# A two-layer hybrid decoder step: cache copies behind the weights of the last layer's feed-forward, the decoded tokens' old conv columns packed into rows before their store

## The chip, the core and the metric

The kernel runs on one core of a Trainium2 chip. The metric is the device time of one execution in microseconds (us). A core has a matrix engine (TensorE, PE in the profile; its weight loads are listed apart as PEld), a vector engine (VectorE, DVE), a scalar engine (ScalarE, ACT), a general engine (GpSimd, POOL) and a sync engine (SyncE, SP), which issues this kernel's transfers to 16 DMA engines. Each engine works through its own list of instructions in order; what it issues to a queue is served beside it. Operands lie in the on-chip SBUF (128 partitions), products are summed up in PSUM, inputs and outputs lie in DRAM.

## The reference, cut to what matters

Two layers work on 1048 tokens: 16 meta tokens and a prompt of 1024, and eight sequences that decode one token each. The numbers are float32.

```python
def decoder_layer(x, lp, st, prompt):
    hn = rmsnorm(x, lp['ln1'])
    q, k, v, u, z, xbc, dtr = split(hn @ lp['w_in'])   # dtr: four columns
    o_att, nk, nv = ...            # window attention over 128 keys; a decoded token's come from the caches
    y5, s5r, s5i = s5_scan(u, ...)                     # S5 state space
    xbc, nconv = causal_conv(xbc, conv0, w, bias)      # four taps; the state is the last three columns
    yc, hssd = ssd_scan(xs, softplus(dtr + bias), ...) # Mamba-2 SSD
    x = x + concat(norm(o_att), norm(y5), norm(yc)) @ lp['w_out']
    return x + (silu(h2 @ wg) * (h2 @ wu)) @ wd        # h2 = rmsnorm(x, lp['ln2'])
# outputs of a decoded token, per layer:
#   k_s, v_s: the cache without its oldest key and value, and the new one
#   conv_s:   the two newer of the three old conv columns, and the new one
```

The older part of k_s and v_s (`o_ko`, `o_vo`: 127 of 128 rows of 128 numbers, for eight sequences and two layers) and of conv_s (`o_convo`: two columns of 512 features for eight sequences, per layer) is only copied from inputs.

## The kernel before, in words

Features lie on partitions, tokens on columns. The tokens are cut into two halves of 528 and 520 columns (`TH`), each half into chunks of 264 and 264 or 256 (`CH`). The program calls the two halves' phases of each layer in an interleaved order: projections and feed-forward (`in_proj`, `out_proj`, `ffn`), which keep PE full, beside the mixers (`attn`, `s5`, `ssd`).

A matrix of weights comes as tiles of 128 x 1024 numbers, 0.52 MB. `weights` loads one into `wr` (two buffers); ACT casts it to `wh` and DVE subtracts to get the rest, `wl` (lines 181 and 183; three buffers each). `mm3` (lines 203 to 210) makes each product in three passes: high part by high part, by low part, and low part by high part, so 24 matmuls a chunk in a projection. For the four columns of dt both parts of the weights share one pass (`weights_dt`), 16 matmuls a chunk.

`load` (line 118) issues every transfer, in or out, on SP, so all stand in one queue. The code's order isn't the order on the engines: a scheduler places each instruction by its dependencies and priority, the weight loads with a priority that lets them go ahead.

At the start the eight tiles of the residual `x` are loaded in chunks (`load_x`); ACT squares them (line 222, `add_square`), the squares are summed, and for the norm factor ACT copies a PSUM row out (line 230, `rstd_sum`). Each product of the first projection is multiplied by this factor on DVE (line 344 in `in_proj`, 348 for other tiles), which frees its PSUM buffer for PE.

The decoded tokens' conv state of a layer is loaded as `cst8` (line 835), 128 partitions of 4 tiles x 8 sequences x 3 columns, in the half that holds the decoded tokens; `ssd` uses it and line 864 stores its newer two columns as they lie there: 4 x 8 x 128 = 4096 runs of two numbers. `ssds` (line 913) is a small tile of `ssd`, copied by DVE before a product with it.

The cache copies (four `load` calls near the program's end, just ahead of the last two `ffn` calls) go from DRAM to DRAM, four in all, each eight rows of 127 x 128 numbers, 65 KB a row. They depend on nothing, and the scheduler places them at the start, ahead of the loads of x.

`ffn(1, 0, na, between)` is the feed-forward of layer 1, first half: for three groups of hidden tiles (8, 8 and 6), `ffn_up` and then `ffn_down`, which takes eight weight tiles `m` and adds their products to x. The S5 products of layer 1, second half (lines 742 to 757), run beside it; they load matrices from DRAM (`ds5d`).

Of the kernel before, what the change touches and what calls it, by code (L numbers as in the profile page):

```python
# [21 lines left out]
DEPTH = 2  # L22
FH = 2816
NHID = FH // 128
TH = (528, 520)            # columns of the two token halves
T0 = (0, 528)
NPR = (528, 512)           # prompt columns of each half
CH = (((0, 264), (264, 528)), ((0, 264), (264, 520)))
CHN = (((16, 272), (272, 528)), CH[1])      # without the meta tokens
NK8 = (66, 64)             # chunks of eight tokens in each half  # L30
# [5 lines left out]
def build(ctx, tc, A):  # L36
# [25 lines left out]
    def slot():  # L62
        # scratch [128, 528]; while the dense phases leave their tiles free these stand in
        if lend["from"] != "s":
            t = lend["half"]
            if t is not None:
                lend["half"] = None
                return t
            t = lent("hs")
            lend["half"] = t[:, 1].bitcast(F32)  # L70
            return t[:, 0].bitcast(F32)
        return slp.tile([128, 528], F32, tag="s", name=nm("s"))
# [4 lines left out]
    def rounded2():  # L77
        # two of them for operands of one-pass products
        if lend["from"] != "s":
            t = lent("hr")  # L80
            return t[:, 0], t[:, 1]
        return [slp.tile([128, 528], F32R, tag="s", name=nm("r")) for _ in range(2)]

    def together(*jobs):
        # steps of the jobs in turn: (generator, where its scratch comes from, its banks)
        alive = list(jobs)
        while alive:
            for job in list(alive):
                g, lend["from"], lend["psum"] = job
                if next(g, job) is job:  # L90
                    alive.remove(job)
        lend.update({"from": "s", "half": None, "psum": "o"})
# [24 lines left out]

    def load(out, in_):
        nc.sync.dma_start(out=out, in_=in_)  # L119
# [20 lines left out]
    # keys: part of the partitions' half, group, other part  # L140
    kp2 = const([128, 2, 2, 640], "kp2", F32R)
    # states of S5 with their real parts above the imaginary ones
    hz = const([128, 4, 2, 67], "hz")
    sz = const([128, 8, 2, 8], "sz")
    # running sums of SSD: rows of three bfloat16 parts, and what picks one of the rows
# [40 lines left out]
    def weights_dt(l, mi):  # L186
        # only four columns: their second parts stand beside the first ones and share a pass
        raw = wp.tile([128, 8, 128], F32, tag="wr", name=nm("wr"), bufs=2)
        with tc.high_priority(offset=3000):
            load(raw, A["w_in"][l, mi])  # L190
        wh = wp.tile([128, 8, 128], F32R, tag="wh", name=nm("wh"))
        S.copy(wh, raw)
        wl = wp.tile([128, 8, 128], F32R, tag="wl", name=nm("wl"))
        S.copy(wl, raw)
        V.tensor_sub(wl[:, :, 32:36], raw[:, :, 0:4], wh[:, :, 0:4].bitcast(F32))
        return wh, wl
# [36 lines left out]
    def rstd_diag(acc, n, scale):  # L233
        # 1 / sqrt(scale * column sums + eps), tokens on partitions, on the diagonals of squares
# [13 lines left out]
    def rstd_rows(acc, n, scale):  # L248
        # the same on all partitions
        w, dg = rstd_diag(acc, n, scale)  # L250
        ps = pmx()
        PE.matmul(ps[:, :n], ones[0:w, :], dg[0:w, :n], start=True, stop=True)  # L252
        return ps[:, :n]
# [46 lines left out]
    def in_norm(l, hf, new):  # L300
        # the gains go on here, the tokens' factors on the products
# [13 lines left out]
    def in_proj(l, hf, xr, early=0):  # L315
        # early: for so many tiles the banks that attention does not use yet serve too
# [4 lines left out]
        for mi, name in enumerate(MT):  # L321
            w = weights(A["w_in"][l, mi], 8) if name != "dt" else weights_dt(l, mi)
            st = stp.tile([128, 528], F32, tag="st", name=nm("st"))
            for c0, c1 in CH[hf]:
# [38 lines left out]
    S5 = {}  # L363

    def s5_prep(l):
# [69 lines left out]
        # abar and its powers 0..8  # L435
# [28 lines left out]
        # zero-order hold  # L464
# [33 lines left out]
        # unit rotations e^{i 8 phi (k+1)} and the decay of a chunk  # L498
# [42 lines left out]
        # chunk matrices  # L541
# [7 lines left out]
        # rows (group, channel) that meet their own channel, for the direct path  # L549
# [3 lines left out]
        # powers in falling order for the chunk's own states  # L553
# [3 lines left out]
        # the inputs' matrices of a pair of groups, apart  # L557
# [7 lines left out]
        for p in range(0, 8, 2):  # L565
# [46 lines left out]
            # convolution kernel inside a chunk: (distance, channel out) by (group, channel in) ...  # L612
# [7 lines left out]
            if p % 4 == 2:  # L620
                # ... turned, with the direct path, and written once for every step
# [11 lines left out]
        # each row moved on by its own step: from a row to the next the reading starts 16 earlier  # L633
# [7 lines left out]
    def s5(l, hf):  # L641
# [6 lines left out]
        nu = nk + 16 if dec else nk     # columns of a group: chunks, and the decoded tokens in first and in last place  # L648
# [11 lines left out]
        for r in range(2):  # L660
# [43 lines left out]
            if dec:  # L704
                # state of the decoded token
# [74 lines left out]
        # gelu, gate, norm; the columns stay in chunk order until the last step  # L780
# [45 lines left out]
    def ssd(l, hf):  # L826
# [10 lines left out]
        for i, name in enumerate(("xs0", "xs1", "B", "C")):  # L837
# [8 lines left out]
            for j in range(3):  # L846
                a = 0 if hist else 3 - j        # the first columns of a prompt have less history
                V.scalar_tensor_tensor(ac[:, a:NP], xi[:, a + hist - 3 + j:NP + hist - 3 + j],
                                       cw[:, 4 * i + j:4 * i + j + 1], ac[:, a:NP], ALU.mult, ALU.add)
# [13 lines left out]
        if dec:  # L863
            load(A["o_convo"][l], cst8[:, :, :, 1:3])
# [9 lines left out]
        # step sizes, tokens on partitions  # L874
# [39 lines left out]
        # the same as rows, in three parts without a rest  # L914
# [20 lines left out]
        # decay of a whole chunk on the partitions of its group  # L935
# [8 lines left out]
        for c0, nq, bi in blocks:  # L944
# [20 lines left out]
            # decay between tokens of the chunk  # L965
# [50 lines left out]
        # gate and norm  # L1016
# [11 lines left out]
    def ssd_dec(l, X, Bt, Ct, dt, dA, yt):  # L1028
# [8 lines left out]
        # step and decay of each head on its partitions  # L1037
# [42 lines left out]
    def attn(l, hf):  # L1080
# [6 lines left out]
        # keys, rotated; the block before the half stands in front  # L1087
# [10 lines left out]
        # both parts of the keys of a group, each on both halves of the partitions  # L1098
# [51 lines left out]
        def rope(c0, nq):  # L1150
# [11 lines left out]
            # the parts of a group's queries, one above the other  # L1162
# [7 lines left out]
        def geometry(c0, nq, bi):  # L1170
            # key columns [before | own]: number before, first column, number, first mask column
# [8 lines left out]
        def scores(blk, qav, jp):  # L1180
            # heads 4 v + j for two j: one bank for both j of a v
# [33 lines left out]
        def values(blk, ps_, jp, po_):  # L1215
            c0, nq, bi = blk
            nb, k0, nkk, m0 = geometry(*blk)
            # a group's two heads: over the keys before and over the own ones
# [130 lines left out]
    def out_proj(l, hf, seq=range(8), banks=None):  # L1349
        # seq: the parts in the order in which they come; banks: of the mixers, when these have come to their end  # L1350
# [3 lines left out]
        for i in seq:  # L1354
# [4 lines left out]
            if j < 4:  # L1359
                # the gains of attention's norm go on here  # L1360
# [6 lines left out]
        # the first columns of the last features come earlier, for the norm that follows  # L1367
# [38 lines left out]
    def ffn_down(l, hf, hs, grp, ms=range(8)):  # L1406
        g0, g1 = grp
        for m in ms:
            w = weights(A["w_down"][l, m, :, g0:g1, :], g1 - g0)
            for c0, c1 in chunks_of(l, hf):  # L1410
# [5 lines left out]
    def ffn(l, hf, xn, between=None):  # L1416
        for grp in HGROUPS:
# [5 lines left out]
            elif (l, hf) == (DEPTH - 1, 1) and grp is HGROUPS[-1]:  # L1423
                ffn_end(hs, grp)
            else:
                ffn_down(l, hf, hs, grp)

    def ffn_end(hs, grp):
        # the last products, and the final norm chunk after chunk
# [69 lines left out]
    for l in range(DEPTH):  # L1499
        load(A["o_ko"][l], A["ck"][l, :, 1:128, :])  # L1500
        load(A["o_vo"][l], A["cv"][l, :, 1:128, :])
    late = []

# [4 lines left out]
    ffn(1, 0, na, between)  # L1508
# [25 lines left out]
def _host(i):  # L1534
# [16 lines left out]
    # four columns only, the rest of their tile is empty  # L1551
    wcols["dt"] = np.concatenate([wcols["dt"], np.zeros((2, 1024, 124), f)], axis=2)

    def tiles(w, nm_):
        # (L, K, M) -> (L, m tile, k within, k tile, m within)
# [13 lines left out]
    def feat(a, n):  # L1569
        # (L, n*128) -> (128, L, n)  # L1570
# [10 lines left out]
    P["cw"] = i["ssd_conv_w"].reshape(2, 4, 4, 128).transpose(3, 0, 2, 1)   # l j tile p -> p l tile j  # L1581
# [6 lines left out]
    sd = np.tile(i["attn_sinks"], (1, 16)).T               # 128 rows of (b kv r)  # L1588
    P["sinkd"] = sd

    def gn(a):
        # (L, 16 g, 64 n, ...) -> (128 = (g%2, n), L, 8 pairs, ...)
# [8 lines left out]
                          i["s5_c_im"].transpose(0, 1, 3, 2))]     # each 128 L pair c  # L1601
# [3 lines left out]
    # states  # L1605
    st = np.stack([i["state_s5_re"], i["state_s5_im"]], axis=1)     # l e b g n
    st = st.reshape(2, 2, 8, 8, 2, 64).transpose(0, 4, 5, 1, 3, 2)  # l h n e pair b
    r["s5st"] = c(st.reshape(2, 128, 2, 8, 8))
    r["cstate"] = c(i["state_ssd_conv"].reshape(2, 8, 3, 4, 128).transpose(0, 4, 3, 1, 2))
    ss = i["state_ssd"].reshape(2, 8, 2, 2, 64, 64).transpose(0, 2, 3, 4, 1, 5)  # l t h p b n  # L1610
# [6 lines left out]
    # constants of the shapes  # L1617
# [64 lines left out]
```

## Time and profile before

| what | us |
|---|---|
| median of three timed runs | 2535.39 |
| lowest and highest | 2534.82, 2536.57 |
| span of the profiled execution | 2540.2 |
| PE idle in it | 112 |

The profile is of one execution; its own time is the span. A busy matmul is one that the record shows between start and end; the matmuls overlap, so their mean duration is longer than the distance between two. In a timeline, a number in brackets is how long the engine had stood idle before the instruction and what ended that. In windows, each engine has its busy us and its instructions, then the clock granted to PE (1.00 is 2.4 GHz, 0.50 is 1.2 GHz), the busy share of the DMA engines and what they moved; in a short window the DMA share can come out above 1.

In forty equal slices of the span, PE is busy in tenths, and the clock granted to it:

```profile
PE   4899887999999999999999999999999999999998
PEclk7999898999999999999999999999999999999999
```

### The profile page before, as it was taken

What the parts mean: (1) busy time and instruction counts of PE and PEld (TensorE: products, weight loads), DVE (VectorE), ACT (ScalarE), POOL (GpSimd) and SP (SyncE); (2) the same over time, 40 slices, a digit from 0 to 9 for tenths busy, and PEclk for the clock granted to TensorE, in tenths of its full rate; (3) what the DMA queues carried; (4) which work ended last, traced back from release to release, by engine and by line L of the source; (5) the groups of instructions that cost most, each with busy time, mean ns of one, the idle gap of its engine ahead of it and who ended that gap; (6) DMA issues with size and microseconds to landing.
All of it is one profiled execution on the core that took longest, in us unless ns stands there. A gap on an engine that the chain in (4) does not pass through costs nothing.

```text
span 2540.2 us, 49614 instructions
## 1 busy us (share of the span) xinstructions
PE 2428.5 (96%) x19878; PEld 2339.0 (92%) x19878; DVE 1460.9 (58%) x3502; ACT 1052.3 (41%) x2177; POOL 350.8 (14%) x476
## 2 busy tenths in 40 slices
PE   4899887999999999999999999999999999999998
PEld 4898787899999999999999999999999998999997
DVE  4886646665557645665654455666565446434435
ACT  4364633334444443443553343333455335323224
POOL 3521112011111231001200022001110004000000
PEclk7999898999999999999999999999999999999999
DMA  8655345354323624344422233435433232332322
GB/s 175 214 189 153 94 136 70 94 166 139 105 85 111 195 93 144 105 133 119 130 84 92 88 116 117 140 109 158 149 96 92 84 121 91 110 92 92 93 89 78
DMA packets 210645, 301.06 MB, mean 119 GB/s; under 512 B 63840, under 2 KB 140464, under 8 KB 210384
## 3 DMA queue, kind: packets, MB, share of 16 engines
q1 hardware_dynamic: 210416, 297.91, 39.2%
q8 instruction: 156, 2.56, 0.4%
q14 instruction: 73, 0.60, 0.1%
HBM read 255.86 MB, written 46.17 MB: 119 GB/s over the span
## 4 chain that ended last, share of the span: by engine, by line
PE 77%; DVE 9%; issue 5%; DMA 4%; SPq 2%; ACT 2%; POOL 1%; DVEq 0%; POOLq 0%; ACTq 0%
PE pb L208 22%; PE pb L209 22%; PE pb L210 22%; SPq L119 2%; DVE wl L183 2%; PE px L1241 1%; PE px L1196 1%; DVE xn L262 1%; PE px L754 1%; DMA s<-dq 1%; PE px L757 1%; DMA x<-xt 1%; DVE hh L201 1%; PE px L1244 1%; PE px L252 1%
## 5 line engine op out<-in xcount | busy, mean ns | idle before, releaser
L208 PE MATMUL pb<-hh,wh 128*128 128x264 f32 (+1 forms) x3200 | 919.3, 287 | 18.6 <-DVE th L1400 16.1
L209 PE MATMUL pb<-hh,wh 128*128 128x264 f32 (+1 forms) x3200 | 913.3, 285 | 0.8 <-DVE hh L201 0.8
L210 PE MATMUL pb<-hh,wl 128*128 128x264 f32 (+1 forms) x3200 | 911.7, 285 | 0.0
L208 PE MATMUL pb<-hl,wh 128*128 128x264 f32 (+1 forms) x2304 | 666.0, 289 | 43.2 <-DVE st L344 26.1
L209 PE MATMUL pb<-hl,wh 128*128 128x264 f32 (+1 forms) x2304 | 663.2, 288 | 0.6 <-DVE hl L1363 0.4
L210 PE MATMUL pb<-hl,wl 128*128 128x264 f32 (+1 forms) x2304 | 661.0, 287 | 0.0
L208 PEld LDWEIGHTS pb<-hh,wh 128*128 128x128 f32 x3200 | 607.7, 190 | 29.3 <-DVE th L1400 20.2
L181 ACT CAST wh<-wr 128x512 fp32r<-128x512 f32 (+2 forms) x536 | 387.1, 753 | 555.1 <-PE pb L209 512.4
L210 PEld LDWEIGHTS pb<-hh,wl 128*128 128x128 f32 x3200 | 607.3, 190 | 3.5 <-issue 2.7
L209 PEld LDWEIGHTS pb<-hh,wh 128*128 128x128 f32 x3200 | 606.3, 189 | 3.0 <-DVE hh L201 1.1
L183 DVE TENSOR_TENSOR wl<-wr,wh 128x512 fp32r<-128x512 f32 (+2 forms) x536 | 461.1, 882 | 179.0 <-ACT wh L181 172.9
L208 PEld LDWEIGHTS pb<-hl,wh 128*128 128x128 f32 x2304 | 441.1, 192 | 53.2 <-issue 33.0
L209 PEld LDWEIGHTS pb<-hl,wh 128*128 128x128 f32 x2304 | 440.5, 191 | 4.5 <-issue 2.3
L210 PEld LDWEIGHTS pb<-hl,wl 128*128 128x128 f32 x2304 | 440.6, 191 | 1.1 <-issue 0.6
L225 POOL TENSOR_TENSOR sq<-sq,sq 128x264 f32<-128x264 f32 (+1 forms) x142 | 117.4, 832 | 760.1 <-ACT sq L222 661.9
L1414 DVE TENSOR_TENSOR x<-x,pb 128x264 f32<-128x264 f32 (+1 forms) x176 | 74.4, 423 | 176.7 <-PE pb L210 175.8
L200 ACT CAST hl<-th 128x264 fp32r<-128x264 f32 (+1 forms) x176 | 71.8, 408 | 200.6 <-DVE th L1401 200.3
L1401 DVE SCALAR_TENSOR_TENSOR th<-th,pb 128x264 f32<-128x264 f32 (+1 forms) x176 | 74.4, 423 | 136.6 <-PE pb L210 135.8
L222 ACT ACTIVATE sq<-x 128x264 f32<-128x264 f32 (+1 forms) x160 | 63.8, 416 | 137.7 <-DVE x L1379 61.7
L1400 DVE SCALAR_TENSOR_TENSOR th<-th,pb 128x264 f32<-128x264 f32 (+1 forms) x176 | 74.0, 420 | 76.5 <-ACT th L1399 75.9
L1399 ACT ACTIVATE th<-pb 128x264 f32<-128x264 f32 (+1 forms) x176 | 67.7, 384 | 108.5 <-PE pb L210 108.3
L201 DVE TENSOR_TENSOR hl<-th,hl 128x264 fp32r<-128x264 f32 (+1 forms) x176 | 77.7, 442 | 27.8 <-ACT hl L200 27.0
(425 smaller groups left out, 2607.3 us busy)
## 6 DMA issues: line engine op xcount, KB each, us to landing
wr<-w_gate SPq DMA_DIRECT2D x88, 512.0 KB
wr<-w_up SPq DMA_DIRECT2D x88, 512.0 KB
wr<-w_down SPq DMA_DIRECT2D x64, 512.0 KB
wr<-w_in SPq DMA_DIRECT2D x60, 512.0 KB
wr<-w_out SPq DMA_DIRECT2D x32, 512.0 KB
wr<-w_down SPq DMA_DIRECT2D x32, 384.0 KB
x<-xt SPq DMA_DIRECT2D x48, 132.0 KB
s<-ds5v SPq DMA_DIRECT2D x16, 256.0 KB
```

The lines of the kernel that those rows point to most:

```text
L181: S.copy(wh[:, a:b], raw[:, a:b])
L183: V.tensor_sub(wl[:, a:b], raw[:, a:b], wh[:, a:b].bitcast(F32))
L200: S.copy(h, src)
L201: (eng or V).tensor_sub(l, src, h.bitcast(F32))
L208: PE.matmul(ps, wh[:, k, :], ah, start=(k == order[0]), stop=False)
L209: PE.matmul(ps, wh[:, k, :], al, start=False, stop=False)
L210: PE.matmul(ps, wl[:, k, :], ah, start=False, stop=(k == order[-1]))
L225: (eng or G).tensor_tensor(acc[:, :n], acc[:, :n], sq[:, :n], ALU.add)
L1399: S.activation(th[:, :n], pg[:, :n], AF.Tanh, scale=0.5)
L1400: V.scalar_tensor_tensor(th[:, :n], th[:, :n], 1.0, pg[:, :n], ALU.add, ALU.mult)
L1401: V.scalar_tensor_tensor(th[:, :n], th[:, :n], 0.5, pu[:, :n], ALU.mult, ALU.mult)
L1414: V.tensor_add(x[hf][m][:, c0:c1], x[hf][m][:, c0:c1], ps[:, :n])
```

## The change

Three things change in the program. First, `load` hands back its instruction, and the four cache copies are issued from `ffn_down` of `ffn(1, 0, ...)`, each tied behind the load of a weight tile with odd `m` (`tc.issue_after`). Second, the old conv columns are copied by POOL into a small tile of 128 x 64 numbers, and this is stored in 128 whole rows. Third, the narrow projection dt is cut at column 344 in place of 264. Comments are dropped too; line numbers move by two to ten.

```diff
...
+    last = [None]
+
     def load(out, in_):
-        nc.sync.dma_start(out=out, in_=in_)
+        last[0] = nc.sync.dma_start(out=out, in_=in_).ins
+        return last[0]
...
-            for c0, c1 in CH[hf]:
+            for c0, c1 in CH[hf] if name != "dt" else ((0, 344), (344, T)):
...
-            load(A["o_convo"][l], cst8[:, :, :, 1:3])
+            cold = small()
+            G.tensor_copy(cold.rearrange("p (i b j) -> p i b j", i=4, j=2), cst8[:, :, :, 1:3])
+            load(A["o_convo"][l].rearrange("p i b j -> p (i b j)"), cold)
...
-    def ffn_down(l, hf, hs, grp, ms=range(8)):
+    def ffn_down(l, hf, hs, grp, ms=range(8), each=None):
         g0, g1 = grp
         for m in ms:
             w = weights(A["w_down"][l, m, :, g0:g1, :], g1 - g0)
+            if each is not None and m % 2:
+                each(last[0])
...
-    def ffn(l, hf, xn, between=None):
+    def ffn(l, hf, xn, between=None, each=None):
...
-                ffn_down(l, hf, hs, grp)
+                ffn_down(l, hf, hs, grp, each=each)
...
-    for l in range(DEPTH):
-        load(A["o_ko"][l], A["ck"][l, :, 1:128, :])
-        load(A["o_vo"][l], A["cv"][l, :, 1:128, :])
...
+    caches = [(A[f"o_{n}o"][l], A[f"c{n}"][l, :, 1:128, :]) for n in "kv" for l in range(DEPTH)]
+
+    def copy_cache(after):
+        if caches:
+            with tc.issue_after(after):
+                load(*caches.pop(0))
...
-    ffn(1, 0, na, between)
+    ffn(1, 0, na, between, copy_cache)
...
```

What this makes of the engines' lists shows in three places. The first is SP at the start, with the conv state and the S5 state loaded (`cst`, `s5st`), before:

```order
L119 DMA cst_896_4574<-cstate 128x96
L119 DMA s5st_5021<-s5st 128x128
L119 DMA o_ko<-ck 8x16256
L119 DMA o_vo<-cv 8x16256
L119 DMA o_ko<-ck 8x16256
L119 DMA o_vo<-cv 8x16256
L119 DMA o_convo<-cst_896_4574 4096x1x2
L119 DMA x_436<-xt 128x264
L119 DMA x_437<-xt 128x264
L119 DMA x_438<-xt 128x264
L119 DMA wr_801<-w_in 128x1024
```

and after:

```order
L121 DMA cst_896_4574<-cstate 128x96
L121 DMA s5st_5023<-s5st 128x128
L121 DMA x_436<-xt 128x264
L121 DMA x_437<-xt 128x264
L121 DMA x_438<-xt 128x264
L121 DMA wr_801<-w_in 128x1024
L121 DMA x_439<-xt 128x264
L121 DMA x_440<-xt 128x264
L121 DMA x_441<-xt 128x264
L121 DMA x_442<-xt 128x264
L121 DMA wr_861<-w_in 128x1024
L121 DMA x_443<-xt 128x264
```

Copies and store are gone from between the two states and x; the store of layer 0 in its new form stands much further down the list.

The second place is ACT at the start, at the squares of x and the copy that ends the norm factor (line 230, after it 233). Before:

```order
L401 ACTIVATE s_460<-cpack_93 128x8
L403 ACTIVATE s_460<-s_460 128x8
L222 ACTIVATE sq_1660<-x_436 128x264
L222 ACTIVATE sq_1664<-x_437 128x264
L222 ACTIVATE sq_1669<-x_438 128x264
L230 COPY s_210<-px_310 128x264
L222 ACTIVATE sq_1674<-x_439 128x264
```

and after:

```order
L225 ACTIVATE sq_1669<-x_438 128x264
L244 ACTIVATE m_305<-px_301,ceps_97 88x3
L404 ACT_TABLE_LOAD
L404 ACTIVATE s_460<-cpack_93 128x8
L225 ACTIVATE sq_1674<-x_439 128x264
L225 ACTIVATE sq_1679<-x_440 128x264
L406 ACTIVATE s_460<-s_460 128x8
L225 ACTIVATE sq_1684<-x_441 128x264
L225 ACTIVATE sq_1689<-x_442 128x264
L225 ACTIVATE sq_1694<-x_443 128x264
L233 COPY s_210<-px_310 128x264
```

The copy `s_210` stood behind three squares and stands behind all eight.

The third place is SP in the feed-forward of layer 1, first half, with S5's loads (`ds5d`, `ds5w`) and stores of the mixers (`dmix`) between the weights of `ffn_down`. Before:

```order
L119 DMA wr_21788<-w_down 128x1024
L119 DMA wr_21846<-w_down 128x1024
L119 DMA dmix_171<-s_19357 128x520
L119 DMA dmix_172<-s_19358 128x520
L119 DMA s_19756<-ds5d_6209 128x4x128
L119 DMA s_19754<-ds5w_6207 64x4x128 x2
L119 DMA s_19761<-ds5d_6209 128x4x128
L119 DMA wr_21904<-w_down 128x1024
```

and after:

```order
L121 DMA wr_21788<-w_down 128x1024
L121 DMA o_ko<-ck 8x16256
L121 DMA dmix_171<-s_19361 128x520
L121 DMA dmix_172<-s_19362 128x520
L121 DMA s_19760<-ds5d_6211 128x4x128
L121 DMA wr_21847<-w_down 128x1024
L121 DMA s_19758<-ds5w_6209 64x4x128 x2
L121 DMA s_19765<-ds5d_6211 128x4x128
L121 DMA s_19759<-ds5w_6209 64x4x128 x2
L121 DMA wr_21905<-w_down 128x1024
L121 DMA o_ko<-ck 8x16256
```

A cache copy has come behind the second and fourth tile; the two of v follow behind the sixth and eighth in the same way. The store of layer 1, `o_convo`, stood between a load of `ddt` and a weight load (`w_gate`), and is gone from there.

## Rows read from the trace of the kernel before

**Rows 1.** The profile's first part: busy us (share) and instructions by engine.
```profile
PE 2428.5 (96%) x19878; PEld 2339.0 (92%) x19878; DVE 1460.9 (58%) x3502; ACT 1052.3 (41%) x2177; POOL 350.8 (14%) x476
```

**Rows 2.** Waits of PE, whole run: who ended them; total us, count, longest.
```profile
PE pb L208 <- DVE st L344: 26.1, 1, 26.1
...
PE px L939 <- DVE ssds L913: 9.6, 1, 9.6
```

**Rows 3.** Timeline, SP's issues (us from start, duration, line, operation), 14 to 60 us.
```profile
17.56 0.81 SPq L119 DMA_DIRECT2D o_ko<-ck  x1
...
20.52 0.64 SPq L119 DMA_DIRECT2D o_convo<-cst  x1
21.20 25.23 SPq L119 DMA_DIRECT2D x<-xt  x3
```

**Rows 4.** Windows of 1 us: length, PE, PEld, DVE, ACT, POOL, clock, DMA, GB/s.
```profile
19.00:20.00 1.00, 1.00 (x8) 0.89 (x9) 1.00 (x3) 0.99 (x4) 0.37 (x1) 1.00 2.07 763
...
22.00:23.00 1.00, 1.00 (x9) 0.93 (x8) 0.44 (x1) 0.91 (x2) 0.88 (x3) 1.00 7.01 529
...
33.00:34.00 1.00, 0.00 (x0) 0.00 (x0) 0.00 (x0) 0.00 (x0) 0.00 (x0) 1.00 1.41 342
...
37.00:38.00 1.00, 0.00 (x0) 0.00 (x0) 0.00 (x0) 0.00 (x0) 0.00 (x0) 0.50 0.95 398
```

**Rows 5.** Timeline, ACT and DVE, 28 to 60 us; brackets: idle before, releaser.
```profile
54.61 0.42 ACT L222 ACTIVATE sq<-x 128x264 f32<-128x264 f32 x1 [26.01 <-DMA x<-xt]
...
57.72 0.36 ACT L230 COPY s<-px 128x264 f32<-128x264 f32 x1
58.11 1.11 DVE L344 TENSOR_TENSOR st<-pb,s 128x264 f32<-128x264 f32 x2 [27.13 <-ACT s L230]
```

**Rows 6.** Timeline, SP, ACT and PE, 419 to 448 us.
```profile
419.89 0.60 SPq L119 DMA_DIRECT2D o_convo<-cst  x1
421.83 5.36 SPq L119 DMA_DIRECT2D wr<-w_gate  x1
...
444.68 1.14 ACT L181 CAST wh<-wr 128x512 fp32r<-128x512 f32 x2 [14.03 <-DMA wr<-w_gate]
...
447.10 0.39 PE L939 MATMUL px<-ssds,cones 128*64 128x8 f32 x4 [9.61 <-DVE ssds L913]
```

**Rows 7.** Windows around the two stalls, columns as in rows 4.
```profile
32.70:58.90 26.20, 0.05 (x2) 0.04 (x1) 0.79 (x2) 1.53 (x4) 1.48 (x2) 0.54 0.62 100
...
58.90:62.10 3.20, 3.20 (x15) 3.20 (x15) 3.19 (x16) 1.98 (x6) 2.34 (x4) 0.50 1.02 362
...
448.00:451.20 3.20, 3.20 (x17) 3.20 (x16) 1.92 (x10) 0.86 (x4) 0.00 (x0) 0.50 0.39 151
...
56.00:64.00 8.00, 5.11 (x30) 5.14 (x31) 5.88 (x23) 4.51 (x11) 5.64 (x8) 0.62 1.01 357
```

**Rows 8.** Timeline, DVE's split of two weight tiles at the start.
```profile
22.56 1.64 DVE L183 TENSOR_TENSOR wl<-wr,wh 128x1024 fp32r<-128x1024 f32 x1 [1.19 <-ACT wh L181]
...
25.12 1.62 DVE L183 TENSOR_TENSOR wl<-wr,wh 128x1024 fp32r<-128x1024 f32 x1
```

**Rows 9.** Timeline, PE, three issues in a row in the middle.
```profile
1230.50 0.28 PE L208 MATMUL pb<-hh,wh 128*128 128x264 f32 x1
1230.62 0.57 PE L1196 MATMUL px<-ckp,r 128*128 128x144 f32 x4
1231.02 0.33 PE L209 MATMUL pb<-hh,wh 128*128 128x264 f32 x1
```

**Rows 10.** Window in layer 1's feed-forward, first half, columns as rows 4.
```profile
1740.00:1750.00 10.00, 9.73 (x85) 8.98 (x83) 7.71 (x15) 4.32 (x6) 1.24 (x4) 1.00 0.61 190
```

**Rows 11.** Timeline, S5 there: a load on SP, its use on ACT, PE.
```profile
1737.77 0.60 SPq L119 DMA_DIRECT2D s<-ds5d  x1
...
1742.95 1.11 ACT L742 COPY s<-s 128x512 f32<-128x512 f32 x1 [0.72 <-DMA s<-ds5d]
...
1747.60 0.34 PE L757 MATMUL px<-ut,s 128*64 128x64 f32 x4
```

## The prediction

> **What bounds the kernel now.** I read the profile in this order. First the busy shares [rows 1]: PE is busy 2428.5 us of the 2540.2 us span, 96%. So the kernel is bound by TensorE, and a change that makes no product faster can only win where PE stands still, some 112 us in all, or where its clock is low. Second, the list of what PE waited for [rows 2]: two single waits stand out, 26.1 us for a DVE product of line 344 and 9.6 us for a DVE copy of line 913. Together they are a third of all idle time. Third, the queue that issues the DMAs at the start [rows 3]: the four cache copies go out at 17.56 us and after, the store of the old conv columns at 20.52, and then three loads of x take 25.23 us to issue, where the first copy takes 0.81 and the store itself 0.64. Fourth, what the DMA engines moved meanwhile [rows 4]: bursts of about half a megabyte at 19 to 20, 22 to 23, 33 to 34 and 37 to 38 us, where a full queue moves 357 GB/s steadily (last window of [rows 7]). Fifth, the engines that stood behind it [rows 5]: ACT took up a square of x at 54.61 after 26.01 us of waiting for it, so it had stood idle since 28.6, and only after three squares came to the copy of line 230 (57.72) that DVE's line 344 (58.11) needs, and PE needs that.
>
> The second wait is the same store once more, without any cache copy beside it [rows 6]: it is issued at 419.89, the weight load behind it at 421.83 takes 5.36 us to issue, and its data come so late that ACT waits 14.03 us, DVE behind ACT, and PE until 447.10. That separates the two suspects: the store of 4096 runs of two numbers alone holds the queue for some 23 us (421.83 to 444.68).
>
> **The change part by part.**
>
> *The store and the copies leave the start.* Removed are PE's 26.15 us [rows 2, 7] (first window: two matmuls in 26.2 us) and what the clock cost behind it: after the idle stretch the clock was granted 0.50 (1.2 GHz), and 15 matmuls took 3.20 us, where at full clock one of 264 columns is issued every 0.12 us [rows 9]: 3.20 - 15 x 0.12 = 1.4 us. What is late next? The loads of x now go out from 17.56. Three are issued at once; the weight load behind them must wait until DVE has split the weights two tiles earlier, 22.56 + 1.64 = 24.20, the next weight load until 25.12 + 1.62 = 26.74 [rows 8]. The built order puts ACT's copy (line 230, now 233) behind the squares of all eight tiles of x, not of three as before; the eighth load stands behind that second weight load and is issued at 26.74 + 0.4, about 27.2. From 24.20 on, two weight tiles (0.52 MB each) and five parts of x (0.135 MB each) are 1.7 MB, at the 357 GB/s of the last window in [rows 7] 4.8 us, so it lands at about 30. Square, copy and one of two DVE products (0.42 + 0.36 + 1.11 / 2 [rows 5]) put PE's restart at 31.5 to 33, and PE runs out of work at 32.7 anyway. I leave 1 us of idle; the bounds are 0 and, if x lands as late as its queue allows (5 us later), 6. Sum: -26.15 - 1.4 + 1.0 = -26.5 us. DVE, ACT and POOL lose the same stretch, so none of them is ahead that would give it back.
>
> *The second store becomes 128 rows of 256 bytes.* Removed: 9.6 us [rows 2], and 17 matmuls in 3.20 us at clock 0.50 behind it, 3.20 - 17 x 0.12 = 1.2 us [rows 7]. From ACT's cast of the late weights to PE's restart it took 447.10 - 444.68 = 2.4 us [rows 6]; PE's work ahead ended 9.61 us before 447.10, at 437.5, so a weight load that lands before 435, 13 us after its issue, leaves no wait. -10.8 us. Added are two POOL copies of 128 x 64 numbers; POOL is busy 14% of the span [rows 1]. They take one more of eight small buffers: 0, at most 1 us.
>
> *The copies go into the feed-forward of layer 1, first half* (about 1720 to 1780 us). In the order one follows the second, fourth, sixth and eighth weight tile of the first group. PE is busy 9.73 of the 10 us from 1740 [rows 10], so a delay counts in full, if one comes through. Each copy is eight rows of 65 KB. At the start they completed at about 19.7, 22.5, 33.5 and 37.5 us [rows 4]: 3 us for one that is undisturbed, up to 11 us for one with the element store beside it. A late weight tile has 12 us of cover: the second stall shows it, where a load late by some 21 us cost PE 9.6. The loads of the S5 mixer, which the order places right behind the first and third copy, have less: issued at 1737.77, they let ACT start at 1742.95, and PE uses the result at 1747.60 [rows 11], so 1747.60 - 1742.95 - 1.11 = 3.5 us of cover. With 3 us a copy costs nothing, with 11 us 7.5 us twice. I take 1 us, nearest to the undisturbed burst; bounds 0 and 15.
>
> The Trainium skill speaks against this part: "DMA: Bandwidth & Descriptors", section "Why a DMA increments its semaphore by 16 and not by 1", says that a transfer is spread over the largest number of engines up to 16 that divides its outer dimension, here 8, and always the lowest ones. By that, each copy would block half the engines of every load behind it. No run here shows the engines apart. With the page's 27 GiB/s an engine I would estimate 2.3 us for a row, which would cost nothing.
>
> *The narrow projection dt is cut at 344 columns* (a part of the diff that the short description leaves out): 344 + 184 (176 in the second half) instead of 264 + 264 (256). Its 16 matmuls a chunk run in each of four projections. Matmuls of 264 columns go out every 0.12 us, and four of 144 columns take 0.40 us until the next, 0.10 each [rows 9]: fewer columns do not shorten in proportion. In proportion 344 columns take 0.158; with 0.10 to 0.12 for the short one the pair takes 0.258 to 0.278 where it took 0.242: 16 x 4 x 0.016 to 0.036 = 1 to 2.3 us; with the long one below proportion it may be 0. I take 1 us.
>
> The rows set this term, and the Trainium skill would make it none: "TensorE: Matmul & The Clock Gate", section "Back-to-back issue gap", gives 81 ns for 128 columns and 131 ns for 512 in a stream with weight loads. Interpolated, as an estimate, the two chunks would take as long as before; the trace's 0.12 us at 264 columns is above the page's line.
>
> *Reordering.* The removed transfers let the scheduler move PE's, ACT's and DVE's instructions between 60 and 480 us. The number of products is the same. Outside the two stalls PE is idle there for some 40 us, so a shuffle may give or take a few: 0, bounds -8 and +8.
>
> **Sum** against the profiled execution: -26.5 - 10.8 + 1 + 1 = -35.3 us, of the 2540.2 us span 2504.9. The median of the timed runs is 2535.39, 4.8 us below that span; I subtract the same 35.3 us from the median: 2500.1 us, say 2500.
>
> **The rivals.**
>
> *The copies cost PE.* Each behaves as the slow burst did, 11 us, and the S5 loads and the weights behind them come late: 7.5 us twice, and with the two other copies as much again at most: 15 to 30 us are lost again. For it: PE has no idle time there, so nothing absorbs it. Against it: the slow burst stood beside the element store, which is gone. With 20 us: 2500 + 20 = 2520.
>
> *The start refills.* The x loads stay the bottleneck: the copy of line 233 behind eight squares waits for an x that lands 10 to 14 us later, since 16 loads of x and two weight tiles must pass through a queue that was already full at 18 us. For it: ACT's new order. Against it: 3.1 MB at 357 GB/s are 9 us. 2500 + 12 = 2512.
>
> *Slower than before.* Place: the queue in the first group of that feed-forward. A copy holds the queue as long as the element store did; four of them 10 us apart then add up, since each begins before the last is through, and PE, which has nothing to spare, takes 9.6 us or more of each and a slow clock behind it. From 21 us of hold a copy the four cost 4 x 11 = 44 us against the 37 gained: 2542. Against it: the second burst took 3 us.
>
> *It doesn't do what it says.* The copies could be hoisted forward again; the built order shows them behind the weights.
>
> **How the numbers follow.** Main case (both stalls go, copies hidden) 0.73; copies cost PE 0.12; start refills 0.11; slower than before 0.03; no effect 0.01. The predicted time is the main case's. Its own range is 2489 to 2511 (reordering, bounds of x and dt); to leave out no more than 2 in 10 I reach into the refill and copy cases, to 2516. Below 2489 I leave 0.06, above 2516 0.13: most of the copy case and the slower one. What a measurement of this kernel can tell from no change is about 0.2%, 5 us: faster by more 0.95, within 0.02, slower 0.03.
>
> **What would show it.** In the profile after: PE's wait for line 344 (347 now) under 3 us and no slice below full clock at the start; the three x loads issued in under 2 us; no wait of PE of several us at line 939 (now 944); PE's busy share in the copies' stretch unchanged, with no new wait behind ds5d; dt matmuls of 184 columns no further apart than 0.12 us. Wrong would be a wait of PE for x in the first 60 us, or one over 3 us at the S5 products of layer 1.

## The result, and the profile after

The changed kernel takes 2507.76 us (median of 4 runs, 2505.31 to 2512.87), the kernel before 2535.11 (4 runs). The ratio of after to before is 0.9899, with a 95% interval of 0.9883 to 0.9914: some 26 us faster, 22 to 30. The forecast was 2500, 35 us faster, with a range of 2489 to 2516.

The busy shares of the profiled execution, then its DMA packets. In the kernel before the packets were 210645, so 7936 are gone, which is 2 x (4096 - 128): the two stores now go out as 128 rows each.

```profile
PE 2424.8 (97%) x19878; PEld 2336.9 (93%) x19878; DVE 1463.1 (58%) x3502; ACT 1054.2 (42%) x2179; POOL 350.1 (14%) x478
...
DMA packets 202709, 301.06 MB, mean 120 GB/s; under 512 B 55904, under 2 KB 132528, under 8 KB 202448
```

PE's waits after (engine, line, releaser: total us, count, longest), against [rows 2]:

```profile
PE pb L211 <- DVE th L1405: 18.2, 18, 3.1
PE px L255 <- DVE dg L247: 11.9, 7, 3.9
...
PE pb L211 <- DVE st L347: 3.5, 1, 3.5
```

Line 347 (344 before) fell from 26.1 to 3.5 us, and the wait for `ssds` is no longer in the list. The start on SP, ACT and DVE (the timeline, to be read against [rows 3, 5]):

```profile
17.89 1.38 SPq L121 DMA_DIRECT2D x<-xt  x3
...
27.06 0.33 SPq L121 DMA_DIRECT2D wr<-w_in  x1
27.43 5.19 SPq L121 DMA_DIRECT2D x<-xt  x9
```

```profile
32.24 0.42 ACT L225 ACTIVATE sq<-x 128x264 f32<-128x264 f32 x1 [1.47 <-DMA x<-xt]
32.58 0.36 ACT L233 COPY s<-px 128x264 f32<-128x264 f32 x1
...
32.85 3.16 DVE L426 SCALAR_TENSOR_TENSOR s<-s 128x8 f32<-128x8 f32 x10
35.94 1.12 DVE L347 TENSOR_TENSOR st<-pb,s 128x264 f32<-128x264 f32 x2
```

Three loads of x issue in 1.38 us, not 25.23. The last x is squared at 32.24 and ACT's copy runs at 32.58. What is late next is DVE: ten small operations of the S5 preparation (line 426, 3.16 us) stand ahead of line 347 in its list, so PE restarts near 36.7. The remaining wait is made by an order, not by a transfer.

**Where the rest went.** To compare the same work at different times, I counted in each trace the matmuls whose stationary operand is a part of a split weight; there are 17024. The table has the time up to the 400th, from there to the 1600th (the mixers of layer 0's first half among it), from the 2000th to the 2400th (the second stall), from the 10000th to the 12800th (projection, S5 and attention of layer 1's second half, with the cache copies after), and the rest. Numbers are means over the profiles named.

| kernel (profiles) | to 400 | 400 to 1600 | 2000 to 2400 | 10000 to 12800 | rest | span |
|---|---|---|---|---|---|---|
| before (3) | 98.2 | 256.4 | 74.6 | 416.4 | 1693.1 | 2538.8 |
| after (3) | 71.9 | 262.3 | 63.4 | 421.6 | 1691.4 | 2510.6 |
| difference | -26.3 | +5.9 | -11.2 | +5.2 | -1.7 | -28.1 |

Four of the windows behind the table, of the first profile of each (length, then PE, PEld, DVE, ACT, POOL busy, clock granted, DMA share, GB/s). Before:

```profile
0.00:98.52 98.52, 58.91 (x429) 57.40 (x429) 63.88 (x191) 38.97 (x75) 41.62 (x63) 0.83 0.75 186
98.52:355.84 257.32, 236.23 (x1892) 215.16 (x1890) 179.79 (x500) 135.11 (x302) 54.15 (x67) 0.94 0.52 158
421.76:496.75 74.99, 65.38 (x557) 62.09 (x556) 39.54 (x117) 24.74 (x66) 1.37 (x2) 0.93 0.50 69
...
1592.58:2009.37 416.79, 415.78 (x3489) 396.44 (x3488) 248.68 (x625) 177.78 (x374) 38.32 (x64) 0.99 0.39 119
```

After:

```profile
0.00:71.73 71.73, 57.97 (x433) 56.64 (x434) 63.56 (x191) 39.14 (x76) 44.51 (x64) 0.98 0.72 232
71.73:331.11 259.38, 235.71 (x1887) 215.21 (x1886) 180.66 (x500) 134.51 (x301) 51.02 (x66) 0.93 0.52 156
397.28:460.71 63.43, 63.43 (x557) 60.23 (x556) 39.80 (x117) 24.95 (x66) 1.37 (x2) 1.00 0.25 81
...
1553.95:1974.38 420.43, 416.06 (x3490) 397.02 (x3488) 249.14 (x625) 179.75 (x376) 38.97 (x64) 0.98 0.41 123
```

The two stalls gave 37.5 us, as forecast. Some 11 us were lost again in two stretches where the work is the same: in the first PE idles 23.7 us (259.38 - 235.71) where it idled 21.1, in the last 4.4 where it idled 1.0. The experiments ask why.

### The profile page after: what moved, and what is told of

Read it like the earlier page. It is cut to its first block, busy times and chain, and to the rows that moved or that the text cites. A ratio compares the mean times of both kernels' runs of the same rounds, so it can differ in the third digit from the quotient of the medians.

```text
span 2505.9 us, 49615 instructions
## 1 busy us (share of the span) xinstructions
PE 2424.8 (97%) x19878; PEld 2336.9 (93%) x19878; DVE 1463.1 (58%) x3502; ACT 1054.2 (42%) x2179; POOL 350.1 (14%) x478
## 4 chain that ended last, share of the span: by engine, by line
PE 78%; DVE 10%; DMA 5%; ACT 2%; issue 2%; POOL 1%; SPq 1%; DVEq 0%; POOLq 0%; ACTq 0%
PE pb L211 22%; PE pb L212 22%; PE pb L213 22%; DVE wl L186 2%; PE px L1246 1%; DVE xn L265 1%; PE px L1201 1%; PE px L757 1%; SPq L121 1%; PE px L760 1%; DMA s<-dq 1%; DVE hh L204 1%; PE px L255 1%; PE px L1249 1%; PE px L810 1%
## 5 line engine op out<-in xcount | busy, mean ns | idle before, releaser
L203 ACT CAST hl<-th 128x264 fp32r<-128x264 f32 (+1 forms) x176 | 71.9, 408 | 204.2 <-DVE th L1406 203.9
L1405 DVE SCALAR_TENSOR_TENSOR th<-th,pb 128x264 f32<-128x264 f32 (+1 forms) x176 | 74.1, 421 | 74.0 <-ACT th L1404 73.8
```

The lines of the kernel that those rows point to most:

```text
L203: S.copy(h, src)
L1405: V.scalar_tensor_tensor(th[:, :n], th[:, :n], 1.0, pg[:, :n], ALU.add, ALU.mult)
```

## The experiments

Each kernel was profiled once, and where a median is given also timed beside the kernel before on the same chip. Diffs are against the kernel before, unless said.

**How far executions differ.** The kernel before, twice more:

> The kernel before again, for a second profile of it. Theory: its waits at the start (26 us) and at line 939 (9.6 us) are the same, and what differs between executions is how long the clock is at 1.2 GHz while PE works: 80 to 110 us in all, each us of it worth half a us. Rival: the wait at the start varies by 5 us or more between executions, and the profile read first was a long one.

> A third profile of the kernel before, as c0_before: theory, both waits within 1 us of the first profile, spans apart by half of the difference in slow-clock time; rival, waits apart by several us.

Spans 2539.1 and 2537.0, against 2540.2 first. Waits of PE in the second profile, then in the third:

```profile
PE pb L208 <- DVE st L344: 24.4, 1, 24.4
...
PE px L939 <- DVE ssds L913: 6.4, 1, 6.4
```

```profile
PE pb L208 <- DVE st L344: 27.5, 1, 27.5
PE px L939 <- DVE ssds L913: 9.5, 1, 9.5
```

The stalls move by up to 3 us from one execution to the next, which falls between theory (1 us) and rival (5 us). The changed kernel, twice more:

> The changed kernel again, beside its variants on one chip. Theory: the profile's lead of 34 us over the profiled execution of before overstates the gain by some 7 us, since that one execution of before (span 2540.2) was long; the timed ratio stays at 0.989 to 0.990 and the span at 2503 to 2511. Rival: the first comparison was low by chance; the ratio comes out at 0.986 to 0.987, as the 34 us say.

> The changed kernel, a third profile and more times. Theory: products 10000 to 12800 again 421 to 424 us, products 400 to 1600 259 to 267 us depending on how long the clock is slow, ratio 0.989 to 0.991. Rival: the stretches differ from the two profiles by more than that, so that no part of the loss belongs to the program.

The ratios were 0.9898 (0.9878 to 0.9918) and 0.9902 (0.9889 to 0.9916), the spans of the profiled executions 2518.1 and 2507.9. So the 34.3 us between the two profiles read first overstate the gain; three profiles of each give 28.1, and the times 25 to 26. Both ratios are as the theories had them; the first span is above its 2503 to 2511. One execution of the same program was 12 us longer than another, and most of that is PE being busy longer (2434.1 against 2424.8 us), at a lower mean clock (0.975 against 0.980). Its stretch 400 to 1600, against the after window above:

```profile
72.65:339.64 266.99, 242.03 (x1886) 220.45 (x1885) 180.74 (x500) 134.39 (x301) 52.46 (x66) 0.91 0.51 152
```

PE is busy 242.0 us there instead of 235.7 with the same instructions, at a granted clock of 0.91 instead of 0.93.

**The store alone.** Only the packed rows; copies and dt as before:

```diff
-            load(A["o_convo"][l], cst8[:, :, :, 1:3])
+            cold = small()
+            G.tensor_copy(cold.rearrange("p (i b j) -> p i b j", i=4, j=2), cst8[:, :, :, 1:3])
+            load(A["o_convo"][l].rearrange("p i b j -> p (i b j)"), cold)
```

> Only the old conv columns are packed into rows; the cache copies stay at the start ahead of the loads of x, and dt is cut as before. Theory A (the store's 4096 short runs hold the queue, the copies are only data): the copies' 2 MB delay x by 6 to 8 us against the full change, the wait of PE at line 347 is 8 to 12 us instead of 3.5, the second stall is gone; 2511 to 2516 us. Rival B (the copies' eight rows of 65 KB are the main block): PE's wait at the start stays at 18 us or more, 2520 to 2526 us.

2513.98 us, ratio 0.9899 (0.9878 to 0.9920). Theory A holds: as far as these intervals tell, the store alone brings the change's whole measured gain. PE's wait, and the windows to the 400th and the 1600th product:

```profile
PE pb L211 <- DVE st L347: 9.0, 1, 9.0
```

```profile
0.00:79.23 79.23, 58.66 (x433) 57.56 (x434) 63.64 (x186) 39.63 (x76) 41.23 (x64) 0.94 0.72 237
79.23:344.72 265.49, 239.29 (x1886) 217.26 (x1885) 180.26 (x505) 140.35 (x305) 52.95 (x66) 0.92 0.50 151
```

With the four copies ahead of x, PE waits 9.0 us instead of some 3.

**The copies alone.** Only the copies moved, by the `each` of the change (left out below); the short runs stay:

```diff
-    for l in range(DEPTH):
-        load(A["o_ko"][l], A["ck"][l, :, 1:128, :])
-        load(A["o_vo"][l], A["cv"][l, :, 1:128, :])
+    caches = [(A[f"o_{n}o"][l], A[f"c{n}"][l, :, 1:128, :]) for n in "kv" for l in range(DEPTH)]
+    ...
+    ffn(1, 0, na, between, copy_cache)
```

> Only the cache copies are moved into the feed-forward; the store of 4096 runs of two numbers stays at both places, and dt is cut as before. Theory A: the store alone, which held the queue for about 23 us at the second place, lets x land at about 41 us, so PE waits 8 to 12 us at the start, and the second stall of about 10 us stays; 2517 to 2523 us. Rival B: without the copies PE waits under 5 us at the start, 2510 to 2515 us.

2540.05 us, ratio 1.0011 (1.0002 to 1.0020): no gain, if anything a loss. Both numbers were missed, theory A's by 17 us or more. Waits of PE, and the windows to the 400th and the 1600th product:

```profile
PE px L255 <- DVE dg L247: 25.1, 9, 14.0
...
PE px L942 <- DVE ssds L916: 8.8, 1, 8.8
...
PE pb L211 <- DVE st L347: 4.0, 1, 4.0
```

```profile
0.00:89.72 89.72, 61.46 (x433) 59.34 (x434) 65.23 (x196) 39.29 (x76) 42.02 (x64) 0.87 0.76 189
89.72:353.08 263.36, 238.31 (x1886) 217.61 (x1885) 179.28 (x495) 138.00 (x303) 52.77 (x66) 0.93 0.50 152
```

The stall has only changed its name: a new wait of 14.0 us at line 255, a product of the norm factor, then 4.0 at line 347. Of 98.2 us to the 400th product 8.5 are gained, and the next stretch loses 7. The second stall stays. A second profile:

> Only the cache copies moved, a second profile. Its twelve timed runs had a median of 2540, the one profile 2534.95 with waits of 14.0 and 4.0 us at the start. Theory: the profile caught a short stall; this one shows 18 us or more of wait at the start, and the copies' move is worth nothing as long as the store stands there. Rival: the waits are again 18 us together, against 26 in before, and the 8 us are lost to a longer slow clock later.

Waits of 15.9 and 3.3 us at the start, 89.7 us to the 400th product, 268.9 to the 1600th. The 19.2 us fit both texts, but the same 89.7 us twice speak for the rival: the first was not a short stall caught by chance. What the copies' move gains at the start is given back behind it, only in part to the clock: of the 12.5 us more than before, PE is busy longer in some 5 (241.2 us at 0.92, against 236.1 at 0.94) and idles longer in the rest.

**Number of runs.** One store halved, the other issued twice:

```diff
-            load(A["o_convo"][l], cst8[:, :, :, 1:3])
+            if l == 0:
+                load(A["o_convo"][l][:, 0:2], cst8[:, 0:2, :, 1:3])
+            else:
+                load(A["o_convo"][l], cst8[:, :, :, 1:3])
+                load(dram([128, 4, 8, 2], "cx"), cst8[:, :, :, 1:3])
```

> The kernel before with its store of short runs changed in number alone: for layer 0 (at the start) only two of four feature tiles are stored, 2048 runs of two numbers; for layer 1 (second place) the store of 4096 runs is issued twice, the second into a scratch tile. Half of layer 0's old conv columns is left out of the output. Theory A (hold in proportion to the runs, some 23 us for 4096): PE's wait at the start falls from 26 to 13 to 17 us, the one at line 942 rises from 9.6 to 30 to 36 us. Rival (a store costs a fixed time, or the bytes count): 24 to 27 us and 9 to 13 us.

Waits of PE, and SP's issues at the second place, against [rows 6]:

```profile
PE px L946 <- DVE ssds L920: 25.5, 1, 25.5
PE pb L211 <- DVE st L347: 15.5, 1, 15.5
```

```profile
416.74 4.80 SPq L121 DMA_DIRECT2D dcx<-cst  x1
421.59 18.59 SPq L121 DMA_DIRECT2D wr<-w_gate  x1
```

Half the runs: 15.5 us, as theory A said. Twice the runs: 25.5, less than its 30 to 36, and far above the rival's 9 to 13. The waits go with the size of the store. That runs count in it and not bytes is shown by the store alone, where the same 32 KB went out in 128 rows and the second wait was gone. 4096 more runs add 25.5 - 8.5 (mean of three profiles of before) = 17 us here, and at the start 26.0 - 9.0 (store alone) = 17 us as well. The 23 us that the prediction took for the hold end only when the weight load behind the store has landed, so they are not the store's alone.

**The order.** The built order of PE in the store alone differs from before in 508 rows (rows that a comparison puts on one side only, buffer numbers left out). Counted in the traces, the copies alone, the half-and-double kernel and the change without the dt cut differ by about as much. The next kernel takes the short runs away and nearly leaves the order as it was (27 rows): the older columns come as an input of their own in the output's layout, and both stores are copies of whole rows from DRAM to DRAM, issued at the start.

```diff
-            load(A["o_convo"][l], cst8[:, :, :, 1:3])
+            load(A["o_convo"][l], A["cold"][l])
```

> The kernel before with one edit: the older conv columns also come as an input of their own in the output's layout, and each layer's store is one copy of 16 rows of 512 numbers from DRAM to DRAM, issued at the start. Copies and dt stay as before, and the built order of PE differs from before in 27 rows, against 508 where the same columns are stored from a packed tile. Theory (what the change loses again between products 400 and 1600, 256 us before, 259 to 267 in variants without the short runs at the start, comes from the new order): that stretch stays at 255 to 259 us, the first 400 products take 78 to 81 us, the second stall is gone; 2503 to 2510 us. Rival (the loss follows from the stall's absence, whatever the order): 262 us or more in that stretch, 2512 to 2517 us.

2509.82 us, ratio 0.9894 (0.9879 to 0.9909). PE's wait at the start, and the windows to the 400th and the 1600th product:

```profile
PE pb L211 <- DVE st L347: 10.0, 1, 10.0
```

```profile
0.00:80.08 80.08, 59.69 (x433) 58.35 (x434) 63.07 (x186) 39.19 (x76) 42.00 (x64) 0.89 0.72 235
80.08:335.68 255.60, 236.11 (x1887) 215.95 (x1885) 181.35 (x505) 134.48 (x301) 54.34 (x66) 0.94 0.52 157
```

The stretch takes 255.6 us, as in before, where the store alone took 265.5 with the same stall ahead of it (10.0 and 9.0 us). That is one profile of each, but they don't stand alone: the four profiles with the old order (three of before, this one) have 255.6 to 257.3 us in this stretch, and the ten of kernels with a new order 259.4 to 268.9, the half-and-double kernel (267.5) among them, which has its long transfers still at the start. What is lost between 400 and 1600 thus belongs to the order the scheduler makes once the transfers at the start change. Then the copies behind the loads of x, in the same kernel:

```diff
+            xl = last[0]
...
+    with tc.issue_after(xl):
+        for l in range(DEPTH):
+            load(A["o_ko"][l], A["ck"][l, :, 1:128, :])
+            load(A["o_vo"][l], A["cv"][l, :, 1:128, :])
```

> As the run before this one, and the four cache copies are tied behind the sixteen loads of x of the first projection (issued at about 36 us). The built order of PE differs from before in 608 rows. Theory: the first 400 products take 72 to 75 us, since nothing stands ahead of x, and the new order loses 4 to 8 us between products 400 and 1600; 2505 to 2511 us. Rival: the copies delay the loads of keys and S5 matrices behind them, which PE waits for; 2513 us or more.

2507.77 us, ratio 0.9886 (0.9873 to 0.9900), span 2503.9: 71.8 us to the 400th product, 266.6 to the 1600th (10 us lost, more than the 4 to 8 expected). Beside it on the same chip the changed kernel had 2510.71 and 0.9902 (0.9889 to 0.9916). The intervals overlap: a version that beats the change is not shown.

**The dt cut.** The change with dt cut at 264, against the full change:

```diff
-            for c0, c1 in CH[hf] if name != "dt" else ((0, 344), (344, T)):
+            for c0, c1 in CH[hf]:
```

> The change without the cut of dt at column 344. Theory: the long and the short chunk cost 0.3 us more in each of four projections, so this is 1 to 1.5 us faster than the full change. Rival: the cut also moves the order of other work, and the difference is several us either way.

> The change without the cut of dt, a second time, beside the full change. Theory: products 10000 to 12800 take 416 to 418 us here and 421 to 424 with the cut, whose new order there costs 5 us; with 0.3 us of matmuls in each projection this is 3 to 7 us faster in the median. Rival: the times agree within 2 us, as in the first comparison, because other stretches give it back.

0.9901 (0.9884 to 0.9919) and 0.9906 (0.9891 to 0.9921), beside 0.9898 and 0.9902 with the cut: no difference in the times. Both theories, faster by 1 to 1.5 and by 3 to 7 us, are not borne out by the medians (2513.26 against 2512.28, and 2512.06 against 2510.71 with the cut); the second rival, within 2 us, is. The matmuls of dt in one undisturbed projection, from the first to the next product, before and then after:

```profile
1018.43:1022.33 3.90, 3.90 (x35) 3.90 (x33) 3.17 (x5) 2.70 (x4) 0.26 (x1) 1.00 0.37 101
```

```profile
979.86:984.12 4.26, 4.26 (x34) 4.26 (x33) 3.54 (x6) 2.75 (x4) 0.32 (x1) 1.00 0.37 117
```

They cost 0.36 us more. The stretch 10000 to 12800 takes 417.0 and 417.5 us without the cut, 420.4, 423.5 and 421.0 with it, as the second theory said; its order of PE differs from before nearly three times as much, counted in the traces. What gives it back is less sure: the cut has the lower mean to the 400th product (71.9 against 73.8) and from 400 to 1600 (262.3 against 264.8), but the single profiles overlap in both.

## Why the prediction was right, and where it was too large

**The start** was priced at -26.5 us and measured at -26.3 (98.2 to 71.9), partly by luck, from parts that were each off. In the first profile of each, PE's wait for line 347 fell by 22.6 us and not by 25.15, since PE was to idle 1 us and idles 3.5. The last x was squared at 32.24, where it was to land at about 30, but that is not what PE waited for: DVE's ten S5 operations came first, which the sum hadn't. The clock gave 0.9 us and not 1.4 (PE busy 58.0 us in the stretch instead of 58.9), and behind the 3.5 us of idle it stood at 0.50 again, against the sign that no slice at the start would be below full clock:

```profile
38.00:41.00 3.00, 3.00 (x15) 3.00 (x15) 3.00 (x28) 0.00 (x0) 0.54 (x1) 0.50 0.42 135
```

Against all this, PE's two waits for DVE's line 348 in this stretch were 5.7 us and are 2.5 (line 351 after), which the sum hadn't either. The rival in which the start refills, at 12 us, didn't come: x was some 2 us late, and DVE's list set PE's restart.

**The second store** was priced at -10.8 and measured at -11.2. This term stood on the cleanest evidence in the profile of before: the same store, with no copy beside it [rows 6].

**The copies in the feed-forward** were priced at 1 us, bounds 0 to 15. From 1685 to 1750 us, in which all four are issued, PE is busy throughout:

```profile
1685.00:1750.00 65.00, 65.00 (x599) 61.99 (x599) 34.56 (x82) 19.77 (x28) 6.90 (x19) 0.89 0.63 178
```

ACT waits 9.7 us for `ds5d` there (9.0 before, from 1722 to 1787), and PE for nothing. Without the dt cut, products 10000 to 12800 take 417.3 us with the copies in them (two profiles) and 415.2 without (store alone, order kept): up to 2 us. Both rivals in which the copies cost PE fall. That half of the DMA engines is blocked by each copy, as the Trainium skill's rule would have it ("DMA: Bandwidth & Descriptors", section "Why a DMA increments its semaphore by 16 and not by 1"), can be read from the packets at the start of the kernel before, where the store of 4096 runs stood right behind the copies. From 21.5 to 29 us, from 29 to 39.5 and from 39.5 to 46.5:

```profile
DMA packets 2072, 0.54 MB, mean 72 GB/s; under 512 B 2064, under 2 KB 2064, under 8 KB 2064
DMA packets 34, 1.07 MB, mean 101 GB/s; under 512 B 16, under 2 KB 16, under 8 KB 16
DMA packets 2064, 0.02 MB, mean 2 GB/s; under 512 B 2064, under 2 KB 2064, under 8 KB 2064
```

Half of the runs go at once, then hardly anything but rows of the copies starts, and the other half goes when the last copy's rows end (39.7 to 40.7). In no run are more than eight of the copies' 32 rows in transit together, and in the copies alone, with none at the start, all 4096 runs go between 22.1 and 31.0. The trace doesn't name the engines, so this is inferred from counts and times. It also shows that copies and store delayed each other at the start: a row of a copy took up to 12.5 us there, and 2.4 in the median of the store alone. In the feed-forward of the changed kernel a row takes up to 3.9 us, and PE waits for none of it.

**The dt cut itself** was priced at 1 us and costs 4 x 0.36 = 1.4, if the other three projections are like the one shown. Its price was taken from the rows. An estimate interpolated from the Trainium skill's figures ("TensorE: Matmul & The Clock Gate", section "Back-to-back issue gap") would have made it none. Here the measurement differs from that estimate: 0.36 us a projection.

**The step that was off is the one on reordering**: 0 us, bounds -8 and +8, between 60 and 480 us alone. It measured +5.9 between products 400 and 1600, inside the bounds but on one side, and +5.2 between 10000 and 12800, where I had looked only at the copies and not at what the dt cut does to the order. The built orders differ in hundreds of rows, and the sum treated that as a shuffle without a sign. Every kernel measured with a new order was slower between 400 and 1600, by 3 to 13 us in single profiles; the one with the order kept was not.

**The base** flattered the sum. I took 35.3 us from an execution of 2540.2 us off a median of 2535.4; the first profile after, 34.3 us shorter, seems to confirm it, but three profiles of each are 28.1 us apart.

**The share of the two parts** is what the prediction didn't ask. It removed "store and copies" as one term. The runs part them: the store carries the gain, and the copies' move alone gives nothing. With the store gone, leaving the copies at the start costs some 5 to 8 us there (79.2 against 73.8 for the change without the cut, 80.1 against 71.8 behind x), which the times don't resolve: 2513.98 with the copies at the start, 2513.26 with them moved.

Why the new orders idle more is open: in the first stretch no single wait is behind it (PE's waits at lines 255, 998 and 1246 are 6.0, 5.2 and 3.0 us in the first profile after, where the same lines, then 252, 993 and 1241, had 4.0, 4.3 and none). In the second it is mostly the wait for `th` at line 1405: 3.1, 2.7 and 3.8 us in the three profiles after, 1.0 in the first before. Why the orders make these waits isn't shown, and the clock, slower in the first stretch in most of the new orders, may follow from the idling or add to it.

## What to carry to other kernels

Count the runs of a transfer, not its bytes: 32 KB in 4096 runs held a queue as long as several weight tiles, and whoever is queued behind it pays. Where a scheduler makes the order, removing a long transfer can rewrite everything behind it, as it did here: price that as a loss with its own term, and test it with a kernel that takes the cost away and keeps the order. Profile the base more than once before a sum is made against its span, and align two traces by counted work, not by time.

## What the runs showed of the hardware that was not expected

The hold of the queue follows the number of runs: 2048 runs of 8 bytes left PE waiting 15.5 us at the start, 4096 left 24.4 to 27.5, and the store in whole rows 9.0, each with the copies ahead of x; at the second place 4096 left 6.4 to 9.6 and 8192 left 25.5. That is 3 to 4 ns a run (6.5 us for 2048, 17 for 4096). The runs themselves are through sooner, at the second place between 421.5 and 433.2 us, but the weight load behind them then moves 2 to 14 of its 4 KB rows a us until 442, where 72 to 76 are seen when nothing disturbs. In the profile after, 512 KB weight loads land in some 3 us:

```profile
wr<-w_gate SPq DMA_DIRECT2D x88, 512.0 KB, 3.2
```

The Trainium skill has what is counted ("DMA: Bandwidth & Descriptors", section "Why a DMA increments its semaphore by 16 and not by 1"): one descriptor moves one contiguous run of the last dimension. The trace agrees, with 7936 packets less for two stores of 4096 runs that became 128 rows each. What a run costs whoever is queued behind it is from the runs here.

The same program differs by up to 17 us between executions on one chip (2503.39 to 2520.20 in six runs of the changed kernel), with granted clocks of 0.975 to 0.981 in the mean. A change of a few us in such a kernel can be read from aligned stretches of several profiles, and hardly from the times.
